# Two product pairs abreast in the prologue of a hybrid decoder layer

## The chip, the cores and the metric

The kernel runs on one core of one Trainium2 chip. The metric is device time in microseconds (us) of one execution, as the median of repeated runs; less is better. A profile is taken of one execution, and the times of single instructions come from it. TensorE is called PE in the profile, VectorE DVE, ScalarE ACT, GpSimd POOL and SyncE SP (SP only issues DMAs here).

## The reference

One decoder layer over 1024 tokens of width 1024, all float32:

```python
h = x * rsqrt(mean(x * x, axis=-1) + 1e-6) * pre_norm_g
proj = h @ w_in                                # 1024 x 1024 by 1024 x 9248
z_ssm, xbc, dt, q, k, v, f, z_att, g_ssm, g_att = split(proj)
a = ssd_scan(silu(causal_conv(xbc)), softplus(dt + dt_bias), ...)   # gated and group-normed with z_ssm
b = forgetting_attention(q, k, v, cumsum(log_sigmoid(f + fgate_b))) * silu(z_att)
merged = sigmoid(g_ssm) * (a @ w_branch_ssm) + sigmoid(g_att) * (b @ w_branch_att)
return x + rmsnorm(merged @ w_out) * post_norm_g
```

Only the beginning matters here: the norm of `x`, the first blocks of `h @ w_in`, and the small columns `dt` and `f`.

## The kernel before

**Products.** A dense product is made a pair of 128-column blocks at a time (class `Pair`), by a scheme with seven half-size products in place of eight. They are numbered 1 to 7. Product n multiplies a weight operand with a data operand. The data operands, by number, are `b11` (1), `b21` (2), `-b22` (3), `t4` (4), `t1` (5), `-t2` (6) and `t3` (7); in the profile they are the tiles x0 (`b11`), x1 (`b21`), x2 (`-b22`), x3 (`t1`), x4 (`-t2`), x5 (`t3`) and x6 (`t4`). They depend on the normed input alone and are made once, in the prologue, four blocks (j) each. The weight operands come from four loaded quarters of the pair (`a11`, `a12`, `a21`, `a22`, tile `raw`) and sums of them (tile `sum`): `s1 = a21 + a22` for product 5, `s2 = s1 + a11` for 6, `a11 + a21` for 7, and `s2 + a12` for 3.

Every operand is split in two float32r parts: ScalarE rounds it (`h`), VectorE subtracts the rounding (`l`). For a weight operand these are L351 (ScalarE) and L352 (VectorE), tile `wop`; for a data operand they are L1179 (ScalarE) and L1181 or L1183 (VectorE), in `put`. A product is 12 matmuls of 512 columns, in two halves of six. Sums of quarters are L357 and L373, on VectorE for these pairs.

**Outputs.** Products 1, 6, 7 and 4 gather in one PSUM bank (tile `pb`), which ScalarE copies out in between (L404, tile `s`); 5 and 3 gather in another (`pc`), 2 has a third (`pd`). VectorE joins banks and copies in `give` (L414, L416, L418).

**Order.** Each engine runs its instructions in the order of its own queue. TensorE's is the program's: `Stream.steps` lists (pair, product), `halves(n)` runs n half products wherever the prologue calls it, and the operand of the step three places further on is prepared just before a step begins. A scheduler sets the order on the other engines when the kernel is built, from priorities; some instructions are pinned. Below, p, q and r are the first three pairs. Steps were p1, q1, p2, q2, p6, p5, p7, p4, p3, q6, q5, q7, r1, q4, q3, and then r2 and on.

**Prologue.** Tokens come in two halves of four tiles (`xt`). `norm_tiles` squares a tile with a row sum (ScalarE L1163; VectorE L1161 for tiles 1 and 3), takes the root (ScalarE L1164) and reciprocal (VectorE L1165), and scales it (VectorE L1167 in the first half, GpSimd L1169 in the second). TensorE then turns the first half's blocks (L133, tile `pt`), which become `low` (L1194, L1196) and the operands x0 and x1, with halves of p1 and q1 in between. A loop over j = 0..3 follows: eight turns of the second half, `up` and `b22` (ScalarE L1214, the latter shown as `b`), four matmuls for `dt` and `f` (tile `df`), the operands x3 and x4, half of p2 or q2, and two subtractions in place (L1228, L1229). Behind it stand x5, x6 and x2, eight half products, and then the next stage: its first VectorE instructions set `ones` (L1254, tile `onesr`) and `summing` (L1270), its first matmuls are `pt_df` on `summing`, and a long chain on VectorE (L679 to L708, tile `t`) makes `dt` and `f` of `pt_df`.

Weight quarters wait in six buffers (`raw`); SP issues their loads (L344) as soon as the quarter before in that buffer has been read for the last time.

Of the kernel before, what the change touches and what calls it, by code (L numbers as in the profile page):

```python
# [16 lines left out]
P = 128  # L17
# [69 lines left out]
def hybrid_layer(ctx: ExitStack, tc, a, out):  # L87
# [234 lines left out]
    class Pair:  # L322
# [7 lines left out]
        def __init__(self, keys, handlers, ops=None, adds=nc.vector):  # L330
            self.keys, self.handlers = keys, handlers
            self.ops = xop if ops is None else ops
            self.adds = adds
            self.raw, self.op, self.prepared = {}, {}, set()
            self.s1, self.sums = None, 0

        def load(self, names):
            for n in names:
                if self.keys[0][0] == "merged":
                    h, t = int(n[2]) - 1, self.keys[int(n[1]) - 1][1]  # L340
                    self.raw[n] = fin["merged"][:, h * KH : (h + 1) * KH, t * P : (t + 1) * P]
                    continue
                t = wp.tile([P, KH, P], F32, tag="raw", bufs=6, name="raw")
                pin(nc.sync.dma_start(t, column_halves(self.keys[int(n[1]) - 1])[int(n[2]) - 1]))  # L344
                self.raw[n] = t

# [5 lines left out]
                nc.vector.tensor_tensor(op[:, 1], src, op[:, 0], ALU.subtract)  # L352
            self.op[which] = op

        def total(self, x, y):
            t = wp.tile([P, KH, P], F32, tag="sum", bufs=2, name="sum")
            self.adds.tensor_tensor(t, x, y, ALU.add)  # L357
            return t

        def prepare(self, which):  # L360
            r = self.raw
            self.prepared.add(which)
            if which in (5, 6) and self.s1 is None:
                self.s1 = self.total(r["a21"], r["a22"])
            if which == 1:
                self.split(1, r["a11"])
            elif which == 2:
                self.split(2, r["a12"])
            elif which == 6:
                self.s2 = self.total(self.s1, r["a11"])  # L370
                self.split(6, self.s2)

                self.adds.tensor_tensor(self.s2, self.s2, r["a12"], ALU.add)  # L373
            elif which == 5:
                self.split(5, self.s1)
            elif which == 7:
                if self.between:
                    self.split(7, self.total(r["a11"], r["a21"]))
                else:

                    self.adds.tensor_tensor(r["a11"], r["a11"], r["a21"], ALU.add)
                    self.split(7, r["a11"])
            elif which == 4:
                self.split(4, r["a22"])
            elif which == 3:
                self.split(3, self.s2)
# [34 lines left out]
        def do(self, which):  # L421
            if which in (2, 4, 3) or which in (5, 7) and self.sums:
                unit, ch = {2: (0, 0), 4: (1, 0), 3: (0, 1)}.get(which, (1, 1))
                for begin in self.handlers[unit][2:]:
                    begin(ch)
            if which == 1:
                pool, tag = self.bank
                self.b = pool.tile([P, HALF], F32, tag=tag, bufs=1, name="pb")
                yield from self.matmuls(self.b, 1, "b11", True)
                self.k1 = self.keep(self.b)  # L430
            elif which == 2:
                pool, tag = self.other
                ps = pool.tile([P, HALF], F32, tag=tag, bufs=1, name="p" + tag)
                yield from self.matmuls(ps, 2, "b21", True)
                self.give(0, 0, ps, self.k1, "sum")
            elif which == 6:
                yield from self.matmuls(self.b, 6, "-t2", False)
                self.k2 = self.keep(self.b)
            elif which in (5, 7):
                if which == 5:  # L440
                    self.c = pj.tile([P, HALF], F32, tag="c", bufs=1, name="pc")
                    yield from self.matmuls(self.c, 5, "t1", True)
                else:
                    yield from self.matmuls(self.b, 7, "t3", False)
                    self.k7 = self.keep(self.b)
                self.sums += 1
                if self.sums == 2:
                    self.give(1, 1, self.c, self.k7, "less")
            elif which == 4:
                yield from self.matmuls(self.b, 4, "t4", False)  # L450
                self.give(1, 0, self.b)
            elif which == 3:
                yield from self.matmuls(self.c, 3, "-b22", False)
                self.give(0, 1, self.c, self.k2, "from")

    class Stream:
# [6 lines left out]
        def __init__(self, pairs, double, last):  # L463
            self.pairs = pairs
            for n, p in enumerate(pairs):
                p.bank, p.other = (pj, "be"[n % 2]), (pjx, "d") if n < double else (pj, "c")

                p.between = n < double or n >= last

            p, q, r = pairs[0:3]  # L470
            self.steps = [(p, 1), (q, 1), (p, 2), (q, 2)] + [(p, n) for n in (6, 5, 7, 4, 3)]
            self.steps += [(q, 6), (q, 5), (q, 7), (r, 1), (q, 4), (q, 3)]
            for n in range(2, last):
                p, nxt = pairs[n], pairs[n + 1]
                self.steps += [(p, i) for i in ((2, 6, 5, 7) if n < double else (6, 2, 7, 5))] + [(nxt, 1)]
# [9 lines left out]
            self.steps += [(h, 6), (h, 5), (h, 7), (h, 2), (h, 3), (h, 4)]  # L485
            self.following = {p: n.ops for p, n in zip(pairs, pairs[1:]) if n.ops is not p.ops}
            self.building = []
            self.chores, self.line = [], []
            self.held = None
            self.count = 0  # L490
# [1 line left out]
            self.run = None  # L492
            self.waiting = []
            self.loads = [(p, names) for p in pairs for names in (("a11", "a12"), ("a21", "a22"))]
            self.loaded = []
            self.load_next()

        def load_next(self):
            p, names = self.loads.pop(0)
            p.load(names)  # L500
            if p.keys[0][0] != "merged":
                self.loaded += [(p, n) for n in names]

        def load_more(self):

# [8 lines left out]
                self.load_next()  # L514

        def begin(self):
            self.load_next()
            self.load_next()
            for p, which in self.steps[:3]:
                self.prepare(p, which)  # L520

        def prepare(self, p, which):
            p.prepare(which)
            self.load_more()

        def after(self, halves, fn):
# [606 lines left out]
    with tc.tile_pool(name="pro", bufs=1, reuse_waits="tile", side="right") as pro, tc.tile_pool(  # L1133
# [23 lines left out]
        def norm_tiles(hf, tiles):  # L1157
            for t, xt in enumerate(tiles, 4 * hf):
                sqt = small("sqt").bitcast(BF16)
                if t in (1, 3):  # L1160
                    nc.vector.tensor_tensor_reduce(sqt, xt, xt, 1.0, 0.0, ALU.mult, ALU.add, ss[:, t : t + 1])  # L1161
                else:
                    nc.scalar.activation(sqt, xt, AF.Square, accum_out=ss[:, t : t + 1])  # L1163
                nc.scalar.activation(rstd[:, t : t + 1], ss[:, t : t + 1], AF.Sqrt, bias=epst, scale=1.0 / D)  # L1164
                nc.vector.reciprocal(rstd[:, t : t + 1], rstd[:, t : t + 1])  # L1165
                if hf == 0:
                    nc.vector.tensor_scalar(xt, xt, rstd[:, t : t + 1], None, ALU.mult)  # L1167
                else:
                    nc.gpsimd.tensor_scalar(xt, xt, rstd[:, t : t + 1], None, ALU.mult)  # L1169
# [14 lines left out]
            return [op.ins for op in made]  # L1184

        tiles = load_tiles(0)
        stream = Stream(order + late + ends, len(order) + 3, len(order) + len(late) + 4)
        norm_tiles(0, tiles)
        tiles2 = load_tiles(1)
        stream.begin()  # L1190
        for k in range(NK):
            pt = turned(tiles, k)
            if k > 1:
                nc.scalar.activation(low[:, k, :], pt, AF.Copy, scale=preg[:, k : k + 1])  # L1194
            else:
                nc.vector.tensor_scalar(low[:, k, :], pt, preg[:, k : k + 1], None, ALU.mult)  # L1196
            put("b11" if k < KH else "b21", k % KH, low[:, k, :])
            if k >= KH:
                stream.halves(1)
        norm_tiles(1, tiles2)  # L1200

# [4 lines left out]
        for j in range(KH):  # L1206
# [11 lines left out]
            with tc.high_priority():  # L1218
# [3 lines left out]
                t2 = small()  # L1222
                nc.vector.tensor_tensor(t2, up[1], t1, ALU.subtract)
                last = put("-t2", j, t2, -1.0)
            stream.halves(1)

            with tc.issue_after(last[1]) if j == KH - 1 else nullcontext():
                nc.vector.tensor_tensor(b11, t2, b11, ALU.subtract)  # L1228
                nc.vector.tensor_tensor(b21, t2, b21, ALU.subtract)  # L1229
        dft = small("dft")  # L1230
        nc.scalar.activation(dft, df, AF.Identity, bias=bdf)
        stream.halves(1)

        with tc.issue_after(last[0]), tc.issue_after(last[1]):
            for j in range(KH):
                put("t3", j, low[:, j, :], order=pin)
        stream.halves(1)
        early.close()
        pools["t4"] = phase_a.enter_context(tc.tile_pool(name="xp4", bufs=1, reuse_waits="tile"))
        xop["t4"] = place(pools["t4"], "t4")  # L1240
        for j in range(KH):
            put("t4", j, low[:, j + KH, :], order=pin)
        stream.halves(1)
        for j in range(KH):
            put("-b22", j, b22[j], -1.0, order=pin)
        stream.halves(5)


# [478 lines left out]
```

## Time and profile before

| | |
|---|---|
| median of 3 runs | 1303.09 us (1302.53 to 1304.8) |
| the profiled execution | 1300.96 us; span from its first to its last instruction 1299.3 us |
| busy in the span | TensorE 1256.0 us (97%), VectorE 1005.9 (77%), ScalarE 792.0 (61%), GpSimd 262.0 (20%) |
| granted TensorE clock | 0.997 of full speed |

Times in the profile are counted from the span's first instruction. In a row of the timeline the first number is the start, the second the duration in us, `xN` how many instructions of a kind follow each other, and in brackets stands how long the engine was idle before and who released it. An instruction's duration contains its way through the engine's pipeline, so the next one often starts before it ends; what an instruction costs its queue is the distance from start to start.

### The profile page before, as it was taken

The numbers are of one execution on the slowest core, as the hardware profiler recorded it, in microseconds if no ns is written. First come the engines' busy times: TensorE is split into PE (matmuls) and PEld (weight loads), VectorE is DVE, ScalarE is ACT, GpSimd is POOL, SyncE is SP. The second block draws the span as 40 slices with busy tenths as digits, with TensorE's granted clock in tenths as the row PEclk, the third lists the DMA queues.
The fourth block names the chain that finished last, engine by engine and source line by source line (L and its number), as shares of the span: only waits on it lengthen the run. The fifth ranks groups of instructions, "written<-read, shape, count | busy, mean of one in ns | idle before, by whom it ended". The sixth has DMA issues, their size and how long they took to land.

```text
span 1299.3 us, 20943 instructions
## 1 busy us (share of the span) xinstructions
PE 1256.0 (97%) x7054; PEld 984.4 (76%) x7054; DVE 1005.9 (77%) x1994; ACT 792.0 (61%) x1738; POOL 262.0 (20%) x250
## 2 busy tenths in 40 slices
PE   5999999999999999999999999999999999899997
PEld 4678778887888888878877777777667777678886
DVE  7989886987888888898676666666787677686975
ACT  7745665566665665566546566566775566653754
POOL 3000440012400340124001121120001001146052
PEclk9999999999999999999999999999999999999999
DMA  8233542645436543655375575666866658556932
GB/s 295 76 107 76 159 146 87 201 145 180 127 120 200 182 131 98 211 167 145 98 229 189 181 232 187 220 222 205 284 225 224 224 184 292 192 181 196 361 112 99
DMA packets 153515, 233.57 MB, mean 180 GB/s; under 512 B 15968, under 2 KB 61504, under 8 KB 153408
## 3 DMA queue, kind: packets, MB, share of 16 engines
q1 hardware_dynamic: 137408, 197.14, 47.7%
q10 hardware_dynamic: 11136, 19.11, 3.9%
q0 software_dynamic: 4864, 15.99, 3.2%
q8 instruction: 55, 0.90, 0.3%
q14 instruction: 52, 0.43, 0.1%
HBM read 162.99 MB, written 72.34 MB: 181 GB/s over the span
## 4 chain that ended last, share of the span: by engine, by line
PE 67%; DVE 12%; ACT 8%; DMA 7%; issue 4%; SPq 1%; POOL 0%; ACTq 0%; DVEq 0%; POOLq 0%
PE pb L130 28%; PE pc L130 15%; PE pd L130 5%; PE av L130 4%; PE pt L133 4%; PE s L130 4%; ACT ex L1468 3%; PE yps L130 2%; DVE wop L352 2%; ACT wop L351 1%; DVE sum L357 1%; DVE xs L771 1%; DVE ex L1464 1%; PE tr L133 1%; DMA xt<-in_x 1%
## 5 line engine op out<-in xcount | busy, mean ns | idle before, releaser
L1468 ACT ACTIVATE ex<-ex,nm 128x512 f32<-128x512 f32 (+1 forms) x192 | 116.0, 606 | 127.9 <-DVE nm L1464 127.8
L352 DVE TENSOR_TENSOR wop<-sum,wop 128x512 fp32r<-128x512 f32 x180 | 136.6, 760 | 56.4 <-ACT wop L351 54.8
L351 ACT ACTIVATE wop<-sum 128x512 fp32r<-128x512 f32 x180 | 112.3, 625 | 84.5 <-DVE sum L357 37.9
L404 ACT ACTIVATE s<-pb 128x512 f32<-128x512 f32 x144 | 85.1, 591 | 94.1 <-PE pb L130 90.9
L352 DVE TENSOR_TENSOR wop<-raw,wop 128x512 fp32r<-128x512 f32 x144 | 102.1, 710 | 45.2 <-ACT wop L351 43.9
L130 PE MATMUL pc<-x3h,wop 128*128 128x512 f32 x384 | 130.5, 397 | 1.7 <-DVE th L414 1.3
L130 PE MATMUL pb<-x0h,wop 128*128 128x512 f32 x384 | 131.2, 398 | 0.0
L130 PE MATMUL pb<-x5h,wop 128*128 128x512 f32 x384 | 129.3, 396 | 1.2 <-ACT s L404 1.2
L130 PE MATMUL pb<-x6h,wop 128*128 128x512 f32 x384 | 129.2, 395 | 1.3 <-ACT s L404 1.3
L130 PE MATMUL pc<-x2h,wop 128*128 128x512 f32 x384 | 130.2, 398 | 0.0
L130 PE MATMUL pb<-x4h,wop 128*128 128x512 f32 x384 | 129.4, 395 | 0.0
L1464 DVE CUSTOM_DVE_ANT_0 ex<-s,fb 128x512 f32<-128x512 f32 (+1 forms) x192 | 95.7, 552 | 34.1 <-PE s L130 34.0
L351 ACT ACTIVATE wop<-raw 128x512 fp32r<-128x512 f32 x144 | 89.6, 623 | 13.9 <-PE pd L130 6.1
L130 PE MATMUL pd<-x1h,wop 128*128 128x512 f32 x288 | 96.3, 394 | 0.0
L130 PEld LDWEIGHTS pc<-x3h,wop 128*128 128x128 f32 x384 | 72.4, 189 | 19.4 <-DVE th L414 1.7
L130 PEld LDWEIGHTS pb<-x5h,wop 128*128 128x128 f32 x384 | 72.1, 188 | 18.8 <-ACT s L404 2.3
L130 PEld LDWEIGHTS pb<-x6h,wop 128*128 128x128 f32 x384 | 72.2, 188 | 17.6 <-ACT s L404 1.7
L130 PEld LDWEIGHTS pc<-x2h,wop 128*128 128x128 f32 x384 | 72.1, 188 | 17.0 <-issue 1.4
L130 PEld LDWEIGHTS pb<-x0h,wop 128*128 128x128 f32 x384 | 72.7, 189 | 16.1 <-issue 0.9
L130 PEld LDWEIGHTS pb<-x4h,wop 128*128 128x128 f32 x384 | 72.1, 188 | 16.1 <-issue 0.9
L133 PE MATMUL pt<-ident,ex 128*128 128x128 f32 x576 | 77.2, 277 | 7.2 <-ACT ex L1468 6.7
L133 PEld LDWEIGHTS pt<-ident,ex 128*128 128x128 f32 x576 | 65.9, 142 | 19.4 <-ACT ex L1468 13.5
(310 smaller groups left out, 2918.8 us busy)
## 6 DMA issues: line engine op xcount, KB each, us to landing
raw<-in_wu SPq DMA_DIRECT2D x128, 256.0 KB
csb<-cs_dram SPq DMA_DIRECT2D x32, 256.0 KB
fb<-f_dram SPq DMA_DIRECT2D x16, 512.0 KB
rb<-st_dram SPq DMA_DIRECT2D x48, 128.0 KB
wd<-in_wo SPq DMA_DIRECT2D x40, 128.0 KB
xt<-in_x SPq DMA_DIRECT2D x8, 512.0 KB
gs_dram<-th ACTq DMA_DIRECT2D x16, 256.0 KB
qh_dram<-th ACTq DMA_DIRECT2D x16, 256.0 KB
```

Of the source, the lines that this page charges most:

```text
L130: return tc.keep_in_program_order(nc.tensor.matmul(*args, **kw))
L133: return tc.keep_in_program_order(nc.tensor.transpose(out_, in_, idn))
L351: nc.scalar.activation(op[:, 0], src, AF.Copy)
L352: nc.vector.tensor_tensor(op[:, 1], src, op[:, 0], ALU.subtract)
L357: self.adds.tensor_tensor(t, x, y, ALU.add)
L404: nc.scalar.activation(s, ps, AF.Copy)
L771: nc.vector.scalar_tensor_tensor(d, u[:, o + j : o + j + HALF], cw[:, tile_idx, j : j + 1], d, ALU.mult, ALU.add)
L1464: nc.vector.tensor_tensor_reduce(o, s[e][:, 0:w], fb[hp, h][:, e, 0:w], 1.0, 3.0e38, ALU.add, ALU.min, nm)
L1468: pin(nc.scalar.activation(o, o, AF.Exp, scale=-1.0, bias=nm, accum_out=hd.at(hd.sm, i, h, e)))
```

## The change

- The steps of p and q go abreast: p1, q1, p2, q2, p6, p5, q6, q5, p7, q7, p3, q3, p4, q4, r1, and then r2 and on as before. The second pair's products 5 and 3 gather in the bank `pd`.
- Three of the first pair's and second pair's tiles get places of their own (`places`): `a11` and `a12` of p, and `s1` of q. The quarters `a11`, `a12` of q are loaded before `a21`, `a22` of p, and one more pair of quarters is loaded at the beginning. For p and q the sum for product 7 is made in place.
- `stream.behind` orders the preparation of weight operands behind the last data operand that was put. Turned blocks and their operands get high priority.
- Tiles 6 and 7 of x are squared by VectorE in place of ScalarE and scaled by VectorE in place of GpSimd.
- `-b22` is put before `t4`.

```diff
@@ class Pair
+            self.third = pj, "c"
+            self.places = {}
+        def place(self, name, tag, bufs):
+            pool = self.places.get(name)
+            if pool:
+                return pool.tile([P, KH, P], F32, name=f"{name}_early")
+            return wp.tile([P, KH, P], F32, tag=tag, bufs=bufs, name=tag)
...
-                t = wp.tile([P, KH, P], F32, tag="raw", bufs=6, name="raw")
+                t = self.place(n, "raw", 6)
...
-                self.s1 = self.total(r["a21"], r["a22"])
+                self.s1 = self.total(r["a21"], r["a22"], "s1")
...
-                    self.c = pj.tile([P, HALF], F32, tag="c", bufs=1, name="pc")
+                    pool, tag = self.third
+                    self.c = pool.tile([P, HALF], F32, tag=tag, bufs=1, name="pc")
@@ class Stream
-                p.between = n < double or n >= last
+                p.between = 1 < n < double or n >= last
...
-            self.steps = [(p, 1), (q, 1), (p, 2), (q, 2)] + [(p, n) for n in (6, 5, 7, 4, 3)]
-            self.steps += [(q, 6), (q, 5), (q, 7), (r, 1), (q, 4), (q, 3)]
+            q.third = pjx, "d"
+            self.steps = [(m, n) for ns in ((1,), (2,), (6, 5), (7,), (3,), (4,)) for m in (p, q) for n in ns]
+            self.steps.append((r, 1))
...
+            self.loads[1:3] = self.loads[2:0:-1]
...
-            self.load_next()
-            self.load_next()
+            for _ in range(3):
+                self.load_next()
...
-            p.prepare(which)
+            with tc.issue_after(self.behind) if self.behind else nullcontext():
+                p.prepare(which)
@@ norm_tiles
-                if t in (1, 3):
+                if t in (1, 3, 6, 7):
...
-                if hf == 0:
+                if t not in (4, 5):
@@ prologue
+        order[0].places = {"a11": pro, "a12": xe}
+        order[1].places = {"s1": xe}
...
+            with tc.high_priority():
...
+                stream.behind = last[1]
                 stream.halves(1)
...
+            stream.behind = last[1]
             stream.halves(1)
...
+        stream.behind = None
...
+        stream.halves(1)
+        for j in range(KH):
+            put("-b22", j, b22[j], -1.0, order=pin)
         stream.halves(1)
         early.close()
...
             put("t4", j, low[:, j + KH, :], order=pin)
-        stream.halves(1)
-        for j in range(KH):
-            put("-b22", j, b22[j], -1.0, order=pin)
         stream.halves(5)
```

More of the change, by code (lines that the diff above doesn't have):

```diff
@@ L353, in split, with total @@
             self.op[which] = op
-        def total(self, x, y):
-            t = wp.tile([P, KH, P], F32, tag="sum", bufs=2, name="sum")
+        def total(self, x, y, name=None):
+            t = self.place(name, "sum", 2)
             self.adds.tensor_tensor(t, x, y, ALU.add)
@@ L487, in __init__ @@
             self.building = []
+            self.behind = None
             self.chores, self.line = [], []
@@ L501, in load_next @@
             if p.keys[0][0] != "merged":
-                self.loaded += [(p, n) for n in names]
+                self.loaded += [(p, n) for n in names if n not in p.places]
         def load_more(self):
@@ L1192, in hybrid_layer @@
             pt = turned(tiles, k)
[L1193 to L1197, printed above, removed]
+            with tc.high_priority():
+                if k > 1:
+                    nc.scalar.activation(low[:, k, :], pt, AF.Copy, scale=preg[:, k : k + 1])
+                else:
+                    nc.vector.tensor_scalar(low[:, k, :], pt, preg[:, k : k + 1], None, ALU.mult)
+                last = put("b11" if k < KH else "b21", k % KH, low[:, k, :])
             if k >= KH:
+                stream.behind = last[1]
                 stream.halves(1)
```

## The prediction

> **What bounds the kernel now.** I read the page first, then the busy time by stretches of the prologue, then who waited for whom between 13 and 60 us, and last VectorE's timeline row by row, because the changed lines all lie in the first 80 us. The page says that TensorE is busy nearly throughout, so a change of order pays only where TensorE waits.
>
> ```profile
> span 1299.3 us, 20943 instructions
> PE 1256.0 (97%) x7054; PEld 984.4 (76%) x7054; DVE 1005.9 (77%) x1994; ACT 792.0 (61%) x1738; POOL 262.0 (20%) x250
> ```
>
> The stretches are: the turned blocks and p1, q1; the loop over j; the eight half products up to `pt_df`; and from there to the beginning of r2. Behind the stretch stand its length and busy us and (instructions) of TensorE, its weight loads, VectorE, ScalarE and GpSimd.
>
> ```profile
> 13.00:28.00 15.00, 13.20 (x62) 10.27 (x61) 13.21 (x21) 14.97 (x33) 12.23 (x4) 1.00 0.92 332
> 28.00:45.00 17.00, 16.91 (x78) 8.36 (x78) 15.66 (x26) 12.09 (x19) 0.00 (x0) 1.00 0.15 48
> 45.00:59.30 14.30, 12.14 (x51) 9.05 (x50) 13.88 (x26) 11.42 (x22) 0.05 (x1) 1.00 0.24 78
> 59.30:79.40 20.10, 20.09 (x93) 16.77 (x94) 18.63 (x42) 9.76 (x19) 1.40 (x2) 1.00 0.35 119
> ```
>
> ScalarE is full in the first stretch (14.97 of 15.00). In the loop TensorE is (16.91 of 17.00). In the third it is VectorE: 13.88 of 14.30, while TensorE has 2.2 us free. From 59.3 on TensorE is full again. What ends last in the third stretch is told by the chain of waits:
>
> ```profile
> 59.01 0.17 DVE onesr L1254
> 59.18 0.09 DVE summing L1270
> 59.31 1.10 PE pt_df L130 x8
> 79.56 2.72 PE pd L130 x12
> ```
>
> TensorE stands at `pt_df` until VectorE has come to `summing`, a tiny instruction that stands in VectorE's queue behind everything the prologue asked of it. From `pt_df` to r2 (`pd` on x1) TensorE runs without a gap. In both versions eight half products stand between the loop and `pt_df`, and the same seven products and the same orders on all engines but for the prologue's remains follow, so the change is worth what it does to the start of `pt_df` plus the waits between it and r2.
>
> **The change part by part: VectorE's queue up to `summing`.** From the first turned block to `summing` VectorE has 8 float32 sums where it had 6, 11 weight operands for 8 (q6, q5, q7 and q3 are new ahead of it, p4 is gone), and 2 joins of banks for 3. That is four instructions of 512 columns more. It also gets two squares and two scalings of 1024 columns. Durations, from start to start:
>
> ```profile
> 7.59 0.75 DVE L1167 TENSOR_SCALAR xt<-xt,rstd 128x1024 f32<-128x1024 f32 x1
> 8.26 0.15 DVE L1165 RECIPROCAL rstd<-rstd 128x1 f32<-128x1 f32 x1
> 9.29 1.21 DVE L1161 CUSTOM_DVE_ANT_0 sqt<-xt 128x1024 bf16<-128x1024 f32 x1
> 10.42 0.75 DVE L1167 TENSOR_SCALAR xt<-xt,rstd 128x1024 f32<-128x1024 f32 x1
> 49.32 1.89 DVE L1181 TENSOR_TENSOR x5l<-low,x5h 128x512 fp32r<-128x512 f32 x3
> 51.13 0.69 DVE L653 SCALAR_TENSOR_TENSOR th<-th 128x512 fp32r<-128x512 f32 x1
> ```
>
> A scaling takes 8.26 - 7.59 = 0.67 us of the queue, a square 10.42 - 9.29 = 1.13, an instruction of 512 columns (51.13 - 49.32) / 3 = 0.60. Together 4 x 0.60 + 2 x 1.13 + 2 x 0.67 = 6.0 us more ahead of `summing`.
>
> What can VectorE regain? It waited in that part of the queue for
>
> ```profile
> DVE th L414 <- PE pd L130: 0.9, 2, 0.5
> DVE x0l L1181 <- ACT x0h L1179: 0.7, 2, 0.4
> DVE sum L357 <- DMA raw<-in_wu: 0.6, 1, 0.6
> DVE x3l L1181 <- ACT x3h L1179: 0.5, 1, 0.5
> DVE wop L352 <- ACT wop L351: 0.2, 1, 0.2
> ```
>
> 2.9 us in all. With more work ahead of each of these, most waits are filled: x0 and the sum (1.3) surely, since ScalarE comes earlier to x0 and the squares stand in the gaps; the bank joins and the weight operand (1.1) partly; the wait of x3 hardly, because ScalarE's table load still stands before it. I take 2.0 of 2.9, with 1.0 and 2.9 as ends. Two rows are far longer than their kind:
>
> ```profile
> 14.12 8.50 POOL L1169 TENSOR_SCALAR xt<-xt,rstd 128x1024 f32<-128x1024 f32 x3 [12.76 <-DVE rstd L1165]
> 17.16 1.45 DVE L357 TENSOR_TENSOR sum<-raw 128x512 f32<-128x512 f32 x1 [0.63 <-DMA raw<-in_wu]
> 18.65 0.69 DVE L357 TENSOR_TENSOR sum<-sum,raw 128x512 f32<-128x512 f32 x1
> 19.78 2.26 DVE L1181 TENSOR_TENSOR x0l<-low,x0h 128x512 fp32r<-128x512 f32 x2 [0.36 <-ACT x0h L1179]
> 21.96 1.28 DVE L352 TENSOR_TENSOR wop<-raw,wop 128x512 fp32r<-128x512 f32 x2
> ```
>
> The sum took 18.65 - 17.16 = 1.49 and the two x0 parts 21.96 - 19.78 = 2.18, so 0.9 and 1.0 too much, each just behind the point where GpSimd ended one of its scalings of 2.83 us (14.12 + 2.83 n is 16.95 and 19.78) and began the next. With two scalings in place of four GpSimd ends at about 19.8, the first coincidence can remain and the second cannot. I take 0.9 off, with 0 and 1.9 as ends. The Trainium skill, "SBUF — State Buffer", section "Who interferes with whom", says that a VectorE instruction with two SBUF inputs and a GpSimd instruction that reads SBUF exclude each other through a shared port, whichever starts first. By it alone both excesses would go with the two scalings, and this step would be 1.0 us better; the trace agrees only in part, since the other rows of VectorE beside GpSimd have their usual 0.7 us.
>
> So `summing` and with it `pt_df` come 6.0 - 2.0 - 0.9 = 3.1 us later (from 6.0 - 2.9 - 1.9 = 1.2 to 6.0 - 1.0 = 5.0). TensorE cannot use its own gains before that point, and they are real:
>
> ```profile
> PE pt L133 <- ACT low L1194: 1.5, 1, 1.5
> PE pb L130 <- ACT s L404: 1.3, 1, 1.3
> PE pt_df L130 <- DVE summing L1270: 0.5, 1, 0.5
> PE pb L130 <- DVE x4l L1183: 0.3, 1, 0.3
> PE pt L133 <- POOL xt L1169: 0.3, 1, 0.3
> 17.89 1.05 ACT L1163 ACTIVATE sqt<-xt 128x1024 bf16<-128x1024 f32 x1
> ```
>
> ScalarE loses two squares of 1.05; one stood right before the `low` that TensorE waited 1.5 for, so p1 begins 1.0 earlier. GpSimd's 0.3 goes. p4 no longer follows p7 on the same bank, so the 1.3 goes. But of the first round's `up` and `b22` the second now stands behind the roundings of p6 and p5 on ScalarE, which wait for VectorE's `s2`, and four matmuls of `df` wait with it: much of the 1.0 is lost there. All this only makes TensorE wait longer at `pt_df`.
>
> Moves that I cost at nothing: the four earlier loads on SP push twelve copies of `w_out` back by two issues, and nothing reads those before the last stage; `-b22` before `t4` puts both before `summing` as before.
>
> **From `pt_df` to r2.** Before, no wait. Now p3 adds to the bank that product 5 left, and must wait until `give` has joined it with p7's copy. In VectorE's new queue that join stands here:
>
> ```
> wop q7 | wop p3 | wop q3 | onesr | summing | cst | sum (r.a21 + r.a22) | sum | copy pt_df x2
> | L684 | L687 | reciprocal | L689 | L690 | L692 | L694 | give p (join) | ...
> ```
>
> (line numbers of before). The sum waits for r's `a22`, whose buffer is q's `a11`, free only after "wop q7"; behind it in the queue wait the copies, the whole chain for `dt`, and the join. The prices:
>
> ```profile
> 62.38 0.80 SPq L344 DMA_DIRECT2D raw<-in_wu  x2
> 66.00 0.69 DVE L357 TENSOR_TENSOR sum<-raw 128x512 f32<-128x512 f32 x1 [0.86 <-DMA raw<-in_wu]
> 66.61 1.74 DVE L688 RECIPROCAL t<-t 128x256 f32<-128x256 f32 x1
> 68.82 0.41 DVE L689 TENSOR_TENSOR t<-t 128x256 f32<-128x256 f32 x1
> 69.27 0.42 DVE L690 TENSOR_TENSOR t<-t 128x256 f32<-128x256 f32 x1
> 61.28 0.48 DVE L679 COPY t<-pt_df 128x128 f32<-128x128 f32 x2
> ```
>
> The second load of that SP row, begun about 62.8, landed at 66.0: 3.2 us. Counting from the end of "wop q7": 3.2, two sums 1.2, copies 0.5, and the chain, where each step waits for the one before, 0.4 + 0.3 (ScalarE's exponential) + 0.3 + 1.7 + 0.45 + 0.45 + 0.3 + 0.4, and the join 0.7: 9.9 us. TensorE comes to p3 after two operands (1.2), the step from `onesr` to `pt_df` (0.3), `pt_df` itself (about 0.9 to its follower) and p7 and q7 (2 x 2.72): 7.8. So p3 waits 2.0 (estimate; 0.3 if the transfer costs nothing, since the copies need `pt_df` anyway, 2.1 at most). q3 waits for its own join too, but that one stands only 2.7 us further on, as TensorE does.
>
> **The sum.** 3.1 + 2.0 = 5.1 us slower, from 1.5 to 7.1. The profiled execution took 1300.96 us for a span of 1299.3; it would become 1306.1. It lay 2.1 under the median of the runs, 1303.09, which would become 1308.2.
>
> **The rivals.**
>
> *Small loss, 0.16.* VectorE regains every wait and both long rows (+1.2), and r's quarter lands in time (+0.3): 1.5 us, 1304.6. For it: GpSimd's contention goes by the rule above. Against: all its terms must fall together.
>
> *Faster, 0.08.* TensorE's gains count: 1.0 at the start, 0.3, 0.3, 1.3 and 0.5, 3.4 us, 1299.7. It decides once VectorE has `summing` ready when TensorE ends q5, 3.4 us before the present 59.2. Against it: VectorE would need to regain 6.0 + 3.4 us and its waits and long rows are 4.8; so a part of the queue would have to run faster than any row of its kind did.
>
> *Larger loss, 0.12.* At `pt_df` TensorE now stands still for some 5 us or more (eight halves end about 45.0 + 4 x 2.72 = 56, `pt_df` starts about 59.3 + 3.1 = 62.4), longer than any wait after its first product. A slow start is seen here:
>
> ```profile
> 18.24 0.77 PE L130 MATMUL pb<-x0h,wop 128*128 128x512 f32 x1
> 20.88 0.60 PE L133 MATMUL pt<-ident,xt 128*128 128x128 f32 x4
> ```
>
> The first six product matmuls took 2.64 us, where later six take half of 2.72. If p7 starts so, 1.3 us are added, but ahead of p3's wait, which hides them unless that wait is short. Unhidden, and with little regained by VectorE (5.0 + 2.1), it makes 7 to 8.4 us, about 1310.8. The Trainium skill, "TensorE: Matmul & The Clock Gate", section "What's actually happening", has the array's clock halved after an idle window of about 3.4 us and restored after a busy one as long; by it the slow start is certain, and about 1.7 us by its figures. The trace has no idle time of that length inside the work to test it.
>
> *The change does not do what it says.* Weight sums go behind data operands in the queue, as said, but with q's operands still ahead of `summing`; that is the forecast itself.
>
> **The numbers.** The forecast's case has 0.64. A measurement of this kernel tells about 0.2%, 2.6 us, from no change. The forecast and the larger loss are slower by more (0.76, and 0.01 of the small one), the small loss lies within (0.15), faster by more is 0.08. The range goes from 1304.0 (the small loss less the spread of the runs) to 1310.6, and leaves out the faster case and half of the larger loss.
>
> **What would show it.** Right: TensorE idle 4 us or more before `pt_df`, released by `summing`, which starts at 61 to 64 us; a second wait of 1 to 2 us at p3's first matmul on x2, released by a VectorE join; r2 (`pd` on x1) at 83 to 86 where it was 79.6; no difference afterwards. Wrong: `summing` before 60, or TensorE not waiting for it, or the shift given back behind r2.

## The result, and the profile after

The changed kernel takes 1307.95 us (median of 10 runs, 1306.12 to 1311.68), the kernel before 1303.88 us beside it (10 runs, 1299.33 to 1307.07). The ratio is 1.0041, with a 95% interval from 1.0024 to 1.0058: slower by 3 to 8 us, 5.3 by the ratio (the two medians lie 4.1 apart). The profiled execution of the changed kernel took 1307.94 us for a span of 1306.2 us.

Lines of code are shifted a little after the change: the sums are L366, VectorE's part of a weight operand L361, of a data operand L1195 and L1197, a join L425. First the page after:

```profile
span 1306.2 us, 20940 instructions
PE 1261.2 (97%) x7054; PEld 988.4 (76%) x7054; DVE 1010.7 (77%) x2000; ACT 791.4 (61%) x1734; POOL 254.4 (19%) x248
```

The shares are those of before to within 1%; a loss of 6 us in one place doesn't show in them. The busy time by stretches does show it (columns as in the prediction: TensorE, weight loads, VectorE, ScalarE, GpSimd, then the granted clock):

```profile
13.00:28.00 15.00, 14.42 (x67) 10.55 (x66) 14.65 (x25) 13.94 (x29) 7.12 (x2) 1.00 1.02 363
45.00:62.40 17.40, 12.22 (x53) 9.46 (x51) 17.40 (x30) 12.89 (x25) 0.00 (x0) 0.96 0.24 79
```

TensorE has 14.42 us of work before 28 us where it had 13.20: it does begin earlier. But in the stretch from 45 us on VectorE is busy for 17.40 of 17.40 us, and TensorE has 5.2 us free. What VectorE does there, the chain that ended last tells, and TensorE's timeline gives the wait:

```profile
62.94 0.08 DVE summing L1290
63.07 1.97 PE pt_df L130 x8
65.04 6.89 PE pb L130 x24
85.55 2.72 PE pd L130 x12
63.07 1.97 PE L130 MATMUL pt_df<-summing,dft 128*128 128x64 f32 x8 [5.16 <-DVE u L771]
```

`summing` comes at 62.86 in VectorE's timeline (59.10 before), `pt_df` at 63.07 (59.31), r2 at 85.55 (79.56). So 3.8 us are lost up to `pt_df` and 2.2 more from there to r2, 6.0 in all. The wait is put down to the instruction after `summing` (`u`, two tiny memsets at 62.97), which is of no account.

`pt_df` takes 1.97 us where it took 1.10, and p7 with q7 6.89 where two products take 2 x 2.72. The granted clock, the third number from the end of a window's row, says why:

```profile
57.90:61.00 3.10, 0.01 (x1) 0.00 (x0) 3.10 (x7) 0.98 (x2) 0.00 (x0) 1.00 0.00 1
61.00:63.10 2.10, 0.03 (x1) 0.03 (x1) 2.10 (x8) 0.22 (x1) 0.09 (x1) 0.50 0.22 32
63.10:67.60 4.50, 4.50 (x15) 3.92 (x16) 2.69 (x8) 0.42 (x1) 0.46 (x2) 0.50 0.14 47
```

3.1 us after TensorE's last matmul, at 61.02 us, the clock was halved, and it came back at 67.84, 4.8 us after `pt_df` began (the bounds are those of the trace's records of the clock).

### The profile page after: what moved, and what is told of

Its sections match the earlier page's. It is cut to its first block, busy times and chain, and to the rows that moved or that the text cites. A ratio compares the mean times of both kernels' runs of the same rounds, so it can differ in the third digit from the quotient of the medians.

```text
span 1306.2 us, 20940 instructions
## 1 busy us (share of the span) xinstructions
PE 1261.2 (97%) x7054; PEld 988.4 (76%) x7054; DVE 1010.7 (77%) x2000; ACT 791.4 (61%) x1734; POOL 254.4 (19%) x248
## 4 chain that ended last, share of the span: by engine, by line
PE 70%; DVE 13%; ACT 6%; DMA 6%; issue 3%; SPq 1%; POOL 0%; ACTq 0%; DVEq 0%; POOLq 0%
PE pb L130 30%; PE pc L130 16%; PE pd L130 5%; PE av L130 4%; PE pt L133 4%; PE s L130 4%; PE yps L130 2%; ACT ex L1488 2%; DVE wop L361 2%; DMA raw<-in_wu 2%; DVE sum L366 1%; PE tr L133 1%; ACT wop L360 1%; DVE ex L1484 1%; DVE xs L785 1%
## 5 line engine op out<-in xcount | busy, mean ns | idle before, releaser
L361 DVE TENSOR_TENSOR wop<-sum,wop 128x512 fp32r<-128x512 f32 x177 | 133.9, 758 | 56.8 <-ACT wop L360 55.1
L361 DVE TENSOR_TENSOR wop<-raw,wop 128x512 fp32r<-128x512 f32 x143 | 103.1, 722 | 44.0 <-ACT wop L360 43.6
```

## The experiments

All times are ratios to the kernel before, run beside it on the same chip, with the 95% interval. "r2" is the start of the first matmul of `pd` on x1 in the timeline of TensorE, 79.39 before and 85.39 in the changed kernel.

### 1: the x tiles alone

Against the kernel before:

```diff
-                if t in (1, 3):
+                if t in (1, 3, 6, 7):
...
-                if hf == 0:
+                if t not in (4, 5):
```

> The kernel before with one part of the change only: VectorE squares and scales tiles 6 and 7 of x; the steps, the sums and all else stay as before. Theory (VectorE's queue up to `summing` sets the start of `pt_df`): 2 x 1.13 + 2 x 0.67 = 3.6 us more in that queue, less the waits that it fills (some 1.3) and one of the two long rows beside GpSimd (0.9): `pt_df` 1.4 us later than before (60.7 instead of 59.3), the kernel 1.4 us slower, ratio about 1.001. Rival A (the loss comes from the new order of the products alone; ScalarE and GpSimd are relieved here): no slower or up to 1 us faster, `pt_df` at 58.3 to 59.3.

Measured: 1.0007 (0.9990 to 1.0024). TensorE's timeline:

```profile
61.51 1.10 PE L130 MATMUL pt_df<-summing,dft 128*128 128x64 f32 x8 [0.54 <-DVE summing L1270]
81.59 0.39 PE L130 MATMUL pd<-x1h,wop 128*128 128x512 f32 x1
```

`pt_df` and r2 come 2.2 us later, more than either side expected. Rival A falls by the trace; the time alone can't tell 0 from 2.2 us.

### 2: the steps alone

Against the changed kernel, the two lines of experiment 1 turned back. What is called the steps alone holds everything else of the change too: the places, the order of the loads, the holding back, the priorities and `-b22` ahead of `t4`.

> The changed kernel without the other part: ScalarE squares tiles 6 and 7 and GpSimd scales them, as before; the new order of the products stays. Theory (VectorE's queue, by the sum of its rows): only 4 x 0.60 = 2.4 us more ahead of `summing` than before, less about 1 of waits filled, so `pt_df` at 60.7 to 61.0, about 2 us earlier than in the changed kernel, and with the wait at p3 the kernel 3 to 3.5 us slower than before, ratio about 1.0025. Rival A (the order of the products alone): as slow as the changed kernel or slower, 5 to 7 us, `pt_df` at 63 or later, because TensorE and ScalarE start later without the relief and VectorE follows them.

Measured: 1.0063 (1.0044 to 1.0082), 8.2 us. Rows of TensorE, and of VectorE's waits between 13 and 66 us (in total, times, longest):

```profile
64.65 1.97 PE L130 MATMUL pt_df<-summing,dft 128*128 128x64 f32 x8 [5.15 <-DVE u L771]
87.11 0.39 PE L130 MATMUL pd<-x1h,wop 128*128 128x512 f32 x1
DVE rstd L1179 <- ACT rstd L1178: 2.6, 1, 2.6
DVE th L423 <- PE pd L130: 1.6, 1, 1.6
DVE x3l L1195 <- ACT x3h L1193: 1.0, 1, 1.0
DVE x1l L1195 <- ACT x1h L1193: 0.5, 1, 0.5
DVE wop L361 <- ACT wop L360: 0.4, 1, 0.4
```

Rival A wins: `pt_df` comes later than 63, and the steps alone cost as much as the whole change or more (r2 is 1.7 us later than in the changed kernel, though the two intervals of the time overlap). By the sum of rows they ask 2.4 us more of VectorE, but `pt_df` moves by 5.3 us. The rest is waiting: 4.5 us of it for ScalarE, against 1.4 before and 1.3 in the changed kernel. Together with experiment 1: the x tiles alone cost 2.2 us at `pt_df`, the steps alone 5.3, both 3.8. The two don't add up; given the steps, the x tiles on VectorE are a gain of 1.6 us there, although they put 3.6 us into its queue.

### 3: `pt_df` without `summing`

```diff
-            mm(pt[:, c * 64 : (c + 1) * 64], dft[:, c * P : (c + 1) * P], summing, start=True, stop=True)
+            for n in range(2):
+                mm(pt[:, c * 64 : (c + 1) * 64], dft[:, c * P : (c + 1) * P], ident[:, 64 * n : 64 * n + 64], start=n == 0, stop=n == 1)
...
-        nc.vector.tensor_tensor(summing, ident[:, 0:64], ident[:, 64:P], ALU.add)
```

> The changed kernel without the tile `summing`: `pt_df` is made by two accumulated matmuls for each of its four parts, on the two halves of `ident` (0.55 us more on TensorE, one VectorE instruction of 0.16 less), so that TensorE waits for nothing of VectorE there. Theory (the debt in VectorE's queue counts, and the copies of `pt_df` with the whole chain for `dt` stand behind it all the same): the wait of 5.2 us at `pt_df` goes, and a wait of some 2 to 4 us comes back on TensorE at a later product that needs the chain or the join; the kernel stays 2 to 4 us slower than before (ratio 1.0015 to 1.003). Rival B (only the place of that one tiny instruction in the queue makes the loss): all of it comes back, as fast as before or up to 1 us faster.

Measured: 1.0045 (1.0025 to 1.0064). TensorE reaches r2 at 79.21, 0.2 us earlier than before, and then stands:

```profile
88.71 0.74 PE L130 MATMUL pt_te<-da,stri 128*128 128x128 f32 x2 [3.90 <-DVE da L723]
90.24 1.89 PE L130 MATMUL pt_cs<-tri,da 128*16 128x128 f32 x8
95.04 1.05 PE L130 MATMUL pt_cs<-tri,da 128*16 128x128 f32 x8
62.64 0.17 DVE L1275 MEMSET onesr<- 128x128 f32 x1
88.28 0.28 DVE L723 SCALAR_TENSOR_TENSOR da<-dtn,ea 128x128 f32<-128x128 f32 x1
```

The last `pt_cs` stood at 89.53 before: 5.5 us late, nearly all of the loss. Rival B falls. The place of the small instruction only decides where TensorE meets VectorE's debt: `onesr` comes 3.6 us later than before (59.01), and `da`, at the end of the chain for `dt`, 4.5 us later (83.78). In the changed kernel, where TensorE had stood still first, `da` came at 82.98, earlier than before. The run is not a pure test, though: with TensorE early, the scheduler put three steps of the next stage (`bt`, 0.75 us each) ahead of `da` that stand behind it in both other kernels. After the wait the clock was at 0.50 again (the first `pt_cs` took 1.89 us for 1.05), which is why it came out worse than the theory's 2 to 4 us: the wait itself is 3.9.

### 4, 5 and 9: keeping TensorE busy in the wait

Ahead of `pt_df`, in the changed kernel, once each:

```diff
+        for c in range(17):                                   # 4
+            mm(pt[:, 256:320], dft[:, 0:P], dft[:, 0:64], start=True, stop=True)
...
+        x7 = xop["t3"][0][:, 0, :]                             # 5
+        for c in range(20):
+            mm(pt, x7[:, 0:P], x7, start=True, stop=True)
...
+        x5, x6 = xop["t3"][0][:, 0, :], xop["t4"][1]           # 9
+        for n, x in ((2, x5), (2, x6[:, 1, :]), (2, x6[:, 3, :])):
+            for _ in range(n):
+                mm(pt, x5[:, 0:P], x, start=True, stop=True)
```

> The changed kernel with 17 small matmuls of 128x64 float32 ahead of `pt_df` (into columns that nobody reads), some 4.7 us of work in the wait of 5.2 us, so that TensorE isn't idle there. Theory (the slow clock after the wait is hidden by the join that p3 needs): the granted clock is 1.00 from 60 to 69 us, `pt_df` starts at the same time, takes 1.1 instead of 2.0 us, p7 runs at full rate, TensorE comes to p3 at about 69.4 and waits there about 2 us for VectorE's join; the kernel as slow as the changed one (ratio to before 1.004, within 0.5 us). Rival C (the slow clock is a loss of its own): 1.3 to 2.3 us faster than the changed kernel, no wait at p3.

Measured: 1.0039 (1.0025 to 1.0054), but the clock fell all the same, so this run decides nothing. The 17 matmuls filled 3.90 us of the wait, 1.42 us stayed idle, and still:

```profile
58.01 3.90 PE L130 MATMUL pt_df<-dft 128*128 128x64 f32 x34
64.00:65.00 1.00, 1.00 (x7) 1.00 (x7) 0.51 (x1) 0.00 (x0) 0.00 (x0) 0.50 0.01 2
```

> The changed kernel with 20 matmuls of a product's own kind (128x512, fp32r, on x of product 7, into the tile of `pt_df`, which `pt_df` then overwrites) in the wait before `pt_df`, some 4.6 us of work: the small matmuls of the run before left the granted clock at 0.5 all the same, so that run told nothing of the clock. Theory (the slow clock is hidden by the join that p3 needs): granted clock 1.00 from 58 to 72 us, `pt_df` 1.1 us, TensorE at p3 by 69.5, a wait there of about 2 us released by VectorE's join, r2 at 85.5 as in the changed kernel, ratio to before 1.004 (as the changed kernel within 0.5 us). Rival C (the slow clock is a loss of its own): r2 at 83.3, no wait at p3, about 2 us faster than the changed kernel, ratio 1.0025.

Measured: 1.0030 (1.0014 to 1.0045). Now the clock held:

```profile
64.00:67.00 3.00, 3.00 (x16) 2.49 (x16) 2.02 (x5) 0.42 (x1) 0.00 (x0) 1.00 0.02 6
69.02 0.63 DVE L425 TENSOR_TENSOR th<-pc,s 128x512 f32<-128x512 f32 x1
83.45 0.39 PE L130 MATMUL pd<-x1h,wop 128*128 128x512 f32 x1
```

r2 is 1.9 us earlier than in the changed kernel, as rival C has it, but not for its reason alone. p's join (second row) begins at 69.02 where it began at 70.85 in the changed kernel: with more matmuls ahead, the scheduler had put it four steps of VectorE's chain forward. Clock and join were taken away together.

> The changed kernel with six matmuls of a product's kind (128x512, fp32r) spread over the wait before `pt_df`: two at once, two behind the second part of `x6l`, two behind its fourth, written into the tile of `pt_df`, which `pt_df` overwrites. Unlike in the run with 20 in a row, all instructions of VectorE, ScalarE and GpSimd keep the order of the changed kernel; there p's join had moved ahead of four steps of the chain for `dt` and came 1.8 us earlier. Theory (slow clock hidden by the join): no idle stretch above 2 us, granted clock 1.00 from 58 to 72, `pt_df` 1.1 us from 63.1, TensorE at p3 by 69.5, a wait of about 2 us there until the join that ends at about 71.5, r2 at 85.3, ratio to before 1.004 as the changed kernel. Rival C (slow clock a loss of its own): no wait at p3, r2 at 83.4, ratio 1.0025 to 1.003.

Measured: 1.0038 (1.0021 to 1.0054); the queues of VectorE, ScalarE and GpSimd were those of the changed kernel. `pt_df` ran at full rate, but the clock fell behind it:

```profile
64.00:67.00 3.00, 3.00 (x9) 2.31 (x9) 2.29 (x6) 0.42 (x1) 0.00 (x0) 0.52 0.02 5
70.63 0.68 DVE L425 TENSOR_TENSOR th<-pc,s 128x512 f32<-128x512 f32 x1
70.86 0.39 PE L130 MATMUL pb<-x5h,wop 128*128 128x512 f32 x1
71.37 0.50 PE L130 MATMUL pc<-x2h,wop 128*128 128x512 f32 x1
85.14 0.39 PE L130 MATMUL pd<-x1h,wop 128*128 128x512 f32 x1
```

The last matmul before p3 began at 70.86, and one follows the other after 0.23 us where nothing is in the way; p3 came 0.51 behind, just after the join had ended at 71.31. So 0.3 us that TensorE had gained were taken by the join. In the changed kernel the join ended at 71.53 and p3 began at 71.77: the two bounds lie on top of each other. No run has the clock at full and the join at its old place, so that the join would have taken all 2 us is argued, not shown.

### 6: p7 ahead of `pt_df`

```diff
-        stream.halves(5)
+        stream.halves(7)
```

> The changed kernel with ten instead of eight half products between the loop and `pt_df`: p7 stands in TensorE's queue before `pt_df`, not after it. VectorE's queue up to `summing` stays as it is, and p's join moves ahead of the copies of `pt_df` in it. Theory (VectorE's queue sets `pt_df`, and the loss is TensorE's idle time and slow clock there plus the join): `summing` at 62.9 as in the changed kernel, the wait at `pt_df` 2.2 to 2.6 us, no slow clock, no wait at p3, r2 at about 80.5; of the loss of 5.3 us some 4 come back there, and up to 3 may go again where TensorE next waits for the chain of `dt` (at `pt_te`); 0.5 to 4 us slower than before, ratio 1.0005 to 1.003. Rival D (VectorE's whole queue, not one point of it, is late, so a wait moved is a wait kept): as slow as the changed kernel, 1.004.

Measured: 1.0012 (0.9997 to 1.0027).

```profile
63.02 1.11 PE L130 MATMUL pt_df<-summing,dft 128*128 128x64 f32 x8 [1.85 <-DVE u L771]
80.42 0.39 PE L130 MATMUL pd<-x1h,wop 128*128 128x512 f32 x1
```

`summing` comes when it came (62.80), the wait shrinks to 1.85 us, the clock holds, and p's join stands ahead of the chain. r2 is 1.0 us later than before instead of 6.0, and no wait comes back at `pt_te`. The theory holds, rival D falls: a queue that is 3.8 us late costs 6.0 or 1.0 us, by what TensorE has to do meanwhile. (`pt_te` now has one product more ahead of it, 2.7 us, and begins 1.5 us after `da` is done.)

### 7: the sums on GpSimd

Experiment 6 and, for p and q:

```diff
+        order[0].adds = order[1].adds = nc.gpsimd
```

> As the run with ten half products ahead of `pt_df`, and the eight weight sums of p and q ahead of it made by GpSimd instead of VectorE (a sum of 128x512 takes some 1.5 us there by its rows, and GpSimd is idle from 22 us on). Theory (VectorE's queue is what sets the time): 8 x 0.60 = 4.8 us leave that queue, `summing` comes at 58 to 59.5, TensorE hardly waits for it, and its own gains from the change (1.0 at the start, 1.3 of p4 behind p7, some 0.5 more) show at last: 1 to 3 us faster than before, ratio 0.998 to 0.999. Rival E (GpSimd's sums, 2.5 times as long and beside VectorE on SBUF, come too late for the weight operands or make VectorE's rows long): VectorE waits for them, `summing` at 61 or later, 2 us slower than before or more.

Measured: 1.0019 (1.0005 to 1.0034). GpSimd's rows, then VectorE's in the same time, and `summing`:

```profile
21.27 1.71 POOL L366 TENSOR_TENSOR sum<-raw 128x512 f32<-128x512 f32 x1
22.95 1.73 POOL L366 TENSOR_TENSOR s_early<-raw 128x512 f32<-128x512 f32 x1
21.77 1.76 DVE L361 TENSOR_TENSOR wop<-raw,wop 128x512 fp32r<-128x512 f32 x1
64.39 0.16 DVE L1291 TENSOR_TENSOR summing<-ident 128x64 f32<-128x64 f32 x1
```

Rival E wins. Eight sums left VectorE's queue, 4.8 us by their rows, and `summing` came 1.6 us later than in experiment 6: a row of 0.68 us took 1.76, about as long as GpSimd's own, and eight rows of VectorE beside GpSimd's sums were long by 7.7 us in all. The Trainium skill, "SBUF — State Buffer", section "Who interferes with whom", has it so: a VectorE instruction with two inputs in SBUF and a GpSimd instruction that reads SBUF lock each other out. Here the trace agrees: the join at 39.39, which has one input in SBUF and one in PSUM, kept its 0.68 us beside a sum.

### 8 and 10: without the holding back

```diff
-            with tc.issue_after(self.behind) if self.behind else nullcontext():
-                p.prepare(which)
+            p.prepare(which)
```

In the changed kernel:

> The changed kernel without the holding back: the operands and sums of the weights may again stand anywhere in VectorE's queue, and not only behind the newest data operand. Steps, early places of the loads and squares of x stay. Theory (holding the sums back left VectorE a gap of 2.6 us between 16.6 and 19.2 us in the kernel with the new steps alone, and the two squares of x fill it in the changed kernel): little is left to gain, `summing` at 62.3 to 63.1, the kernel as the changed one within 1 us, ratio 1.0035 to 1.0045. Rival F (the holding back delays VectorE's queue further on too): `summing` 1.5 us earlier or more, a ratio of 1.0025 or less.

Measured: 1.0042 (1.0025 to 1.0059); `summing` at 61.36, 1.5 us earlier, and r2 at 83.29, 2.1 us earlier. The trace speaks for rival F, the time for the theory, and the interval holds both: not settled.

With the steps alone:

> The kernel with the new steps alone (ScalarE and GpSimd square and scale tiles 6 and 7 as before), and without the holding back of the weights' operands and sums. Theory (the loss of 8.2 us with the new steps alone is the debt of four more instructions, 2.4 us, and 3.1 us more of waits, above all the one of 2.6 us at 16.7, which the held back sum left empty): that wait is filled again, `summing` 1.5 to 2.6 us earlier than 64.4, ratio to before 1.0035 to 1.005 instead of 1.0063. Rival G (the new steps cost it whatever stands in that gap, by the order of the products and the joins): ratio 1.006 or more, `summing` at 64 or later.

Measured: 1.0064 (1.0044 to 1.0084), as with the holding back; `summing` at 65.97. By both rival G wins. But the theory's gap was not filled, and another loss came in. VectorE's rows, then a wait of TensorE and one of ScalarE:

```profile
18.28 0.69 DVE L366 TENSOR_TENSOR sum<-raw 128x512 f32<-128x512 f32 x1 [1.84 <-DMA raw<-in_wu]
DVE x1l L1194 <- ACT x1h L1192: 2.5, 1, 2.5
PE pb L130 <- DVE x0l L1194: 2.7, 2, 1.9
30.99 0.69 ACT L1210 ACTIVATE low<-pt,preg 128x512 f32<-128x512 f32 x1 [1.91 <-PE pt L133]
```

The sum that was to stand in the gap waited 1.84 us for its load. Behind it weight operands and sums now stood ahead of the last two parts of x0, so TensorE waited 2.7 us for these, and its clock was at 0.50 from 24.35 to 31.18 us. ScalarE in turn waited 1.91 us for a block that TensorE turned (last row), and rounded x1 from it right after; so VectorE's wait of 2.5 us for that rounding goes back to TensorE, and not to a full ScalarE. What the gap under the holding back costs with the steps alone stays open.

Why the x tiles on VectorE gain 1.6 us in experiment 2 stays open too. They take two squares (2.1 us) off ScalarE, which was full in the first stretch before (14.97 of 15.00 us), and they fill VectorE's gap of 2.6 us; both go by one edit, and no run separates them.

### 11 and 12: a version better than both

The changed kernel with ten half products ahead of `pt_df` (6), no holding back (8), and tile 7 squared by ScalarE (what this last part is worth by itself was not measured):

```diff
-                if t in (1, 3, 6, 7):
+                if t in (1, 3, 6):
```

> A try at a version better than both: the changed kernel with ten half products ahead of `pt_df`, no holding back of the weights' operands and sums, and tile 7 squared on ScalarE again (1.13 us off VectorE's queue; ScalarE has the time, 13.9 of 15.0 us busy from 13 to 28). Theory (VectorE's queue up to `summing` decides, and each of these takes from it or gives TensorE work in the wait): `summing` at 60.5 to 61.5, hardly a wait at `pt_df`, r2 at 79 to 80, the kernel as before within 1 us, ratio 0.999 to 1.001. Rival D (what is taken away comes back as waits further on): 1.002 or more.

> The version of the last run once more, unchanged, since its interval just touched no change: r2 stood 1.2 us earlier there than in the kernel before, TensorE waited for VectorE nowhere between the loop and r2 but 0.4 us at p3. Theory (the time follows r2 one to one): ratio to before 0.9991, between 0.998 and 1.0. Rival D (the gain at r2 is given back later, or the first measurement was chance): 1.0 or more.

Measured: 0.9986 (0.9971 to 1.0001), and in the second measurement 0.9978 (0.9961 to 0.9995): 1.8 to 2.9 us faster than before, with one of the two intervals touching no change.

```profile
59.93 0.16 DVE L1289 TENSOR_TENSOR summing<-ident 128x64 f32<-128x64 f32 x1
60.15 1.10 PE L130 MATMUL pt_df<-summing,dft 128*128 128x64 f32 x8
78.22 0.39 PE L130 MATMUL pd<-x1h,wop 128*128 128x512 f32 x1
```

There is no wait at `pt_df` any more, and r2 is 1.2 us earlier than before: TensorE's earlier start counts once VectorE is in time.

### All runs by one row

A shift of r2 by x us should change the time by x of 1301 us. For experiment 3, which waits later, the second `pt_cs` is taken.

| kernel | shift, us | ratio by it | measured |
|---|---|---|---|
| x tiles alone (1) | +2.2 | 1.0017 | 1.0007 (0.9990 to 1.0024) |
| steps alone (2) | +7.7 | 1.0059 | 1.0063 (1.0044 to 1.0082) |
| changed kernel | +6.0 | 1.0046 | 1.0041 (1.0024 to 1.0058) |
| without `summing` (3) | +5.5 | 1.0042 | 1.0045 (1.0025 to 1.0064) |
| 17 small matmuls (4) | +6.9 | 1.0053 | 1.0039 (1.0025 to 1.0054) |
| 20 wide matmuls (5) | +4.1 | 1.0031 | 1.0030 (1.0014 to 1.0045) |
| p7 earlier (6) | +1.0 | 1.0008 | 1.0012 (0.9997 to 1.0027) |
| sums on GpSimd (7) | +3.2 | 1.0025 | 1.0019 (1.0005 to 1.0034) |
| not held back (8) | +3.9 | 1.0030 | 1.0042 (1.0025 to 1.0059) |
| six wide matmuls (9) | +5.8 | 1.0044 | 1.0038 (1.0021 to 1.0054) |
| steps alone, not held back (10) | +7.4 | 1.0057 | 1.0064 (1.0044 to 1.0084) |
| better version (11) | -1.2 | 0.9991 | 0.9986 (0.9971 to 1.0001) |
| the same again (12) | -1.0 | 0.9992 | 0.9978 (0.9961 to 0.9995) |

Each interval holds the ratio that the one row gives; the intervals reach about 2 us to either side. So as far as they can tell the start of r2 (in experiment 3, the second `pt_cs`) is the change's price. The single traces differ by a few us more behind it: the spans of the two profiled executions lie 6.9 us apart and not 6.0, and in that of the changed kernel the clock was at 0.50 once more from 320.43 to 323.84 us, where it was at 1.00 before.

## Why the prediction was right, step by step

**VectorE's queue.** `summing` 3.8 us later, forecast 3.1 (1.2 to 5.0): right, with terms that were off and in part made up for each other. The work added was as counted, 6.0 us. Of the 2.9 us of waits 0.6 were filled, not 2.0: those for x0, the sum and `wop` went, as forecast, but that for `pd` stayed at 0.9 and that for x3 grew from 0.5 to 1.3, as the first two of these rows show.

```profile
36.61 0.69 DVE L423 TENSOR_TENSOR th<-pd,s 128x512 f32<-128x512 f32 x1 [0.95 <-PE pd L130]
42.24 0.69 DVE L1195 TENSOR_TENSOR x3l<-th,x3h 128x512 fp32r<-128x512 f32 x1 [1.33 <-ACT x3h L1193]
14.80 1.59 DVE L1175 CUSTOM_DVE_ANT_0 sqt<-xt 128x1024 bf16<-128x1024 f32 x1
14.20 7.23 POOL L1183 TENSOR_SCALAR xt<-xt,rstd 128x1024 f32<-128x1024 f32 x2 [12.83 <-DVE rstd L1179]
18.81 2.04 DVE L1195 TENSOR_TENSOR x0l<-low,x0h 128x512 fp32r<-128x512 f32 x2
20.77 1.22 DVE L1181 TENSOR_SCALAR xt<-xt,rstd 128x1024 f32<-128x1024 f32 x1
```

The long rows beside GpSimd did not shrink by 0.9: 1.9 us too much in two rows became about 1.6 in the last three rows of VectorE above (1.59 for 1.21, then from start to start 1.96 for 1.21 and 1.13 for 0.67). The forecast that the coincidence with x0 could not remain was wrong; GpSimd took 7.2 us for its two scalings and not 5.7. Nor could both excesses have gone, as the prediction had it for the rule alone: two scalings still ran beside these rows, until 21.43 us. These two terms were 2.0 us too large together. What met them, some 1.4 us, came out of a third long row (a `wop` of 1.24 us at 24.71 before) and of small gaps of 0.1 to 0.2 us, which the sum did not have: that the total came within 0.7 us is partly luck.

**What the parts are worth.** Here the prediction would have misled. It charged the x tiles with 3.6 us and the steps with 2.4, in one sum. The sum was right for both together; experiments 1 and 2 show 2.2 and 5.3 at `pt_df` for each alone. VectorE waited 4.5 us for ScalarE with the steps alone and 1.3 with both, so a part that loads one engine and frees the other can't be priced in one queue.

**TensorE's gains.** They only lengthened the wait: 5.16 us, forecast 4 or more. Right, and experiment 11 shows them coming through.

**From `pt_df` to r2.** 2.2 us lost, forecast 2.0, but the visible wait at p3 did not come. The two times that the forecast compared were right, counted from the end of "wop q7" (61.52, where the instruction behind the first of these rows begins): the join ended 10.0 us on, forecast 9.9, and TensorE came to p3 10.2 us on, which less the 2.3 us below is 7.9, forecast 7.8.

```profile
60.91 0.68 DVE L361 TENSOR_TENSOR wop<-raw,wop 128x512 fp32r<-128x512 f32 x1
70.85 0.68 DVE L425 TENSOR_TENSOR th<-pc,s 128x512 f32<-128x512 f32 x1
```

The slow clock took 0.87 us of `pt_df` and 1.45 of p7 and q7, 2.3 in all, so TensorE came to p3 0.24 us after the join. This is the mechanism of the rival "larger loss", which the prediction held certain by the Trainium skill ("TensorE: Matmul & The Clock Gate", section "What's actually happening": the clock is halved after an idle window of about 3.4 us and comes back after a busy one); the trace agrees, with the clock halved 3.1 us after the last matmul and at 0.50 for 6.83 us. That the slow clock would lie over the join's wait was said there; that it would cover all of it was not, and the two came out alike by chance.

The slow first product at 18.24 before, which the prediction gave as its sign, bears it out:

```profile
18.00:21.00 3.00, 3.00 (x11) 2.38 (x10) 2.60 (x4) 3.00 (x7) 3.00 (x2) 1.00 1.06 370
19.24 1.05 PE L130 MATMUL pb<-x0h,wop 128*128 128x512 f32 x2
65.80 1.05 PE L130 MATMUL pb<-x5h,wop 128*128 128x512 f32 x2
```

The window's row gives a clock of 1.00, but the trace's records of the clock begin only at 20.78 us, and without a record the row gives 1.00. The matmuls tell more: two of them took 1.05 us at 19.24 (before), as at 65.80 in the changed kernel, where the clock stood at 0.50, and 0.63 from 20.78 on. So TensorE ran its first product at half pace.

**The sum.** 5.1 us forecast; 6.0 at r2, 5.3 by the ratio.

## What to carry to other kernels

Find the one instruction at which the engine that bounds the kernel waits for another engine's queue, and price a change by what it does to that queue. A saving elsewhere is then worth nothing until that wait is gone. Price parts that touch two engines together, and when a wait can't be shortened, give the bounding engine something to do in it: reordering one product took back 5 of 6 us here.

## What the runs showed of the hardware

- The granted clock changes on a raster. In the records of all fourteen traces every stretch between two changes is a whole multiple of 3.41 us (3.41, 6.83, 40.96 and so on), but for the last, which the end of the trace cuts. So the length of a wait alone does not decide: one of 2.84 us (8) lay inside one such stretch, 58.73 to 62.14, and the clock fell at its end; one of 2.85 (10) fell on two, 1.9 us in the first and 1.0 in the second, and the clock stayed at 1.00. One of 1.85 (6) left it at 1.00 too. In experiment 9 it fell 1 us after `pt_df` had begun, with no idle stretch above 1.5 us before.
- Small float32 matmuls did not hold it up in the one run that tried: 34 instructions of 64 columns in 3.90 us (4) and 1.42 us of waiting ended with the clock at 0.50, twenty of 512 columns in 4.70 us and 0.58 of waiting (5) kept it at 1.00.
- A 128x512 sum on GpSimd takes 1.6 to 1.7 us, and VectorE's rows with two inputs in SBUF beside it up to 1.77 instead of 0.68 (7). Beside GpSimd's scalings, with one tensor input, only some rows of VectorE were long (before: 1.45 us at 17.16, but 0.69 at 18.65).
